# Three raw-weight buffers and four chain rows instead of two and five, norm factors spread by transposes, and a channel mean by one product

## The chip, the cores and the metric

The kernel runs on one core of one Trainium2 chip. The metric is the device time of one execution in microseconds (us). The core's engines are named as the profile names them: PE is TensorE's matmuls and PEld its weight loads, DVE is VectorE, ACT is ScalarE, POOL is GpSimd, SP is the engine whose queue issues most of the DMAs.

## The reference, cut to what matters

A decoder trunk of two layers works on 1024 tokens with 1024 channels, all in 32-bit floats. Each layer does, cut to its steps:

```python
a = rmsnorm(h, norm_mix_pre[i])
u = a @ w_in[i]                      # q, k, v, indexer's qi, ki, wi, and the two other groups
y_attn = dsa_sparse_attention(...)   # per query: the 256 best keys by the indexer, softmax over them
y_conv = conformer_conv(...)         # GLU, depthwise conv of 31 taps, LayerNorm, swish, pointwise
y_pool = multiscale_pool(...)
h = h + rmsnorm(concat(y_attn, y_conv, y_pool) @ w_out[i], norm_mix_post[i])
m = relu(rmsnorm(h, norm_mlp_pre[i]) @ w_up[i]) ** 2
h = h + rmsnorm(m @ w_down[i], norm_mlp_post[i])
h = h + sigmoid(h @ ple_gate[i]) * (p[i] @ ple_proj[i])
```

An rmsnorm divides each token by the root of the mean of its squares over 1024 channels. The LayerNorm in `conformer_conv` takes away the mean over 256 channels first.

## The kernel before, in words

Activations lie with channels on the partitions and tokens along the row, so a norm needs a sum over partitions. The tokens are done in two halves of 512. The work is a list of eight phases (layer, half, kind): `win` is the first projection of a half, `m` all from the output projection to the gate. Two things run beside each other in the program.

**The dense stream.** A phase is a run of units. A unit multiplies one block of weights, 1024 x 128, with eight activation tiles (`slot`), each split into a high and a low part, and sums 24 matmuls into one bank (`pd`, a ring of three): high by high (line 243), high by low (248), low by high (249; where activations are fresh, 245 and 246 in the other order). `prepare` fetches the raw weights by DMA into a buffer of the ring `wraw` (line 199, 512 KB on SP's queue), and for each half of the block ACT copies the high part (`whi`, line 204) and POOL subtracts it to get the low part (`wlo`, line 205). `whi` and `wlo` hold four halves each, two units. In an `m` phase eight units of `w_up` fill eight slots, whose split is done by ACT (line 260) and DVE (line 261) after the square (lines 981, 982), and eight units of `w_down` read all eight slots; this happens four times. I call the change from one to the other an up-down edge: the first matmul of `w_down` needs slots that were split a moment ago.

**The chain.** Attention, convolution and pooling of a half run as generators beside the dense units (`run`, `advance`), a share of them for each unit. For the second half of a layer attention goes in three stages. `index` scores the keys. `select` finds the 256th largest score of each query by bisecting, first over the upper and then over the lower 16 bits, 31 steps in all; in each step ACT counts for key blocks 1 and 2 (line 683) and DVE for blocks 0 and 3 (line 669), each count writes flags that nobody reads into a buffer taken from a ring, and DVE then works out the next threshold from the four counts (lines 687 to 689). For the second half that ring is `row`, and two of its buffers hold the packed scores through the whole stage. Then `attend` does softmax and products (transposes on line 789, products with the values on lines 797 and 798), two heads at a time, with the probabilities of two pairs in `row` buffers. The convolution takes its buffers from `row` too. Attention's results go by DMA to `mixS` (line 812); at the start of an `m` phase the chain of that half has been drained, and POOL's queue loads eight slots from `mixS` (line 923).

**The order.** The code says which instructions there are, and which buffer each use gets: a ring hands out the buffer that was put back first. A scheduler with its own model of time then sets the order on each engine, and adds the waits for buffers that are used again. Engines run their instructions in that order.

**Norm factors.** `token_sums` brings the sums of squares onto partitions, one column per 128 tokens (line 298, 128x1 results). A tiny DVE and a POOL instruction make the factor, and `spread` (line 303) brings it back along the row on all partitions, by four products of a broadcast column with the identity. `rms` does all of that. The convolution's mean uses `token_sums`, a DVE scaling (line 551) and `spread`.

Of the kernel before, what the change touches and what calls it, by code (L numbers as in the profile page):

```python
# [8 lines left out]
F32 = mybir.dt.float32  # L9
# [7 lines left out]
OP = mybir.AluOpType  # L17

P = 128
# [67 lines left out]
def tile_trunk(ctx: ExitStack, tc: tile.TileContext, xT, pT, pos, vecs, invf, cinv,  # L87
               win, wout, wup, wdown, wgate, wple, wcp, outT):
    nc = tc.nc
    te, ve, sc, gp, sy = nc.tensor, nc.vector, nc.scalar, nc.gpsimd, nc.sync  # L90
    side = ["dense"]

    const = ctx.enter_context(tc.tile_pool(name="const", bufs=1))
# [26 lines left out]


    slots = Ring("slot", 16, [P, 2, HALF], F32R)
    wraw = Ring("wraw", 2, [P, 8, P])
    whi = Ring("whi", 4, [P, 4, P], F32R)
    wlo = Ring("wlo", 4, [P, 4, P], F32R)
    dtmp = Ring("dtmp", 11, [P, HALF])
    ctmp = Ring("ctmp", 5, [P, HALF])
    cmat = Ring("cmat", 6, [P, HALF], F32R)
    rows = Ring("row", 5, [P, 1088])
    qst = Ring("qst", 2, [P, 4, P], F32R)  # L130
    idx_t = [const.tile([P, (5 + j) * P], F32, name=f"idx{j}") for j in range(4)]
    kd = const.tile([P, 2, S], F32R, name="kd")
# [6 lines left out]
    def tiny(name, n=4, dt=F32, bufs=4):  # L139

        key = name + side[0][0]
        if key not in tinies:
            tinies[key] = [small.tile([P, n], dt, name=f"{key}{i}") for i in range(bufs)]
        tinies[key].append(tinies[key].pop(0))
        return tinies[key][-1]
# [8 lines left out]
    ident = const.tile([P, P], F32, name="ident")  # L154
    ve.tensor_scalar(ident, jp, 0.0, None, op0=OP.is_equal)
    ones = const.tile([P, 1], F32, name="ones")
    ve.memset(ones, 1.0)
    mhalf = const.tile([P, 4], F32, name="mhalf")
    ve.memset(mhalf, -0.5)
    hb = const.tile([P, DEPTH, 2], F32, name="hb")  # L160
# [133 lines left out]
    def token_sums(ps, srcs):  # L294

        for j in range(4):
            for i, src in enumerate(srcs):
                te.matmul(ps[:, j:j + 1], src[:, j * P:(j + 1) * P], ones, start=i == 0, stop=i == len(srcs) - 1)  # L298

    def spread(ps, t4):  # L300

        for j in range(4):
            te.matmul(ps[:, j * P:(j + 1) * P], t4[:, j:j + 1].to_broadcast([P, P]), ident, start=True, stop=True)

    def rms(ps, srcs, n, eps, other=None):

        token_sums(other or ps, srcs)
        v = tiny("rv")
        ve.tensor_scalar(v, (other or ps)[:, :4], 1.0 / n, eps, op0=OP.mult, op1=OP.add)
        r = tiny("rr")  # L310
        gp.tensor_tensor(r, v, mhalf, op=OP.pow)
        spread(ps, r)
# [12 lines left out]
    def win_phase(l, hf, xs, sq):  # L325
# [53 lines left out]
        for name in win_order(l, hf):  # L379
# [14 lines left out]
            elif kind == "P":  # L394
# [4 lines left out]
                if c == 1:  # L399
                    bg.append(((l, hf), conv_pool(l, hf)))  # L400
# [54 lines left out]
    def conv_pool(l, hf):  # L455
# [39 lines left out]
        for c in range(2):  # L495
# [20 lines left out]
            ps = banks.get()  # L516
# [28 lines left out]
        ps = banks.get()  # L545
        both = ctmp.get()
        gp.tensor_tensor(both, acc[:, 0], acc[:, 1], op=OP.add)
        token_sums(ps, [both])
        ctmp.put(both)
        mu = tiny("mu")  # L550
        ve.tensor_scalar(mu, ps[:, :4], 1.0 / 256, None, op0=OP.mult)
        spread(ps, mu)
        sq = [ctmp.get(), ctmp.get()]
        for c in range(2):
            ve.tensor_tensor(acc[:, c], acc[:, c], ps, op=OP.subtract)
# [22 lines left out]
        for o in range(2):  # L578
            ps = banks.get()
# [584 lines left out]
```

## Time and profile before

| what | value |
|---|---|
| time, median of 3 runs | 2843.78 us (2837.95 to 2844.03) |
| time of the profiled execution | 2843.85 us |
| its span, first to last instruction | 2842.1 us |
| PE busy | 2720.5 us, 96% of the span |
| DVE, ACT, POOL busy | 1747.6, 1548.1, 1418.0 us |
| mean granted clock of TensorE | 0.985 of full speed |

Matmuls are pipelined, so the time of one in the profile is longer than the distance to the next, and the busy time counts overlaps once. A clock of 0.50 is TensorE's lower level, 1.2 GHz in place of 2.4.

### The profile page before, as it was taken

Reading aid. Unit: us, or ns where it says so; the run is one execution under the profiler, and the core shown is the slowest. Engines: PE = TensorE matmul, PEld = TensorE weight load, DVE = VectorE, ACT = ScalarE, POOL = GpSimd, SP = SyncE. Lnnn points to the kernel's source line nnn. Section 1 sums busy time; section 2 is a strip of 40 time slices with the busy share of each in tenths; the row PEclk is TensorE's granted clock in tenths of the full one; section 3 lists DMA queues with packets and bytes.
Section 4 is the critical chain, followed back from the end, with each engine's and each line's share of the span. In section 5 each row is a group of like instructions: output and inputs, shape, how many; then the busy total and the mean of one; then the engine's idle time right before and its main releaser. Section 6 shows DMA issues by size and latency. Waiting matters only on the chain.

```text
span 2842.1 us, 37724 instructions
## 1 busy us (share of the span) xinstructions
PE 2720.5 (96%) x12648; PEld 2242.8 (79%) x12648; DVE 1747.6 (61%) x3473; ACT 1548.1 (54%) x2932; POOL 1418.0 (50%) x1161
## 2 busy tenths in 40 slices
PE   7899989999999999899999989999999999999998
PEld 6677777887888878778788777888878878788886
DVE  7969679788447775965822467587985561511123
ACT  5347667775567535766334423677757654533343
POOL 4655425444334665544544755444443356544446
PEclk9999999999999999999999999999999999999999
DMA  5676554422343576533333547534223354423233
GB/s 189 198 192 218 153 134 148 112 85 90 93 115 106 159 238 187 162 116 102 114 104 104 184 152 238 152 116 108 97 79 98 104 164 138 155 97 99 98 97 122
DMA packets 195666, 384.90 MB, mean 135 GB/s; under 512 B 17424, under 2 KB 76944, under 8 KB 195472
## 3 DMA queue, kind: packets, MB, share of 16 engines
q1 hardware_dynamic: 138192, 330.58, 35.7%
q0 software_dynamic: 57280, 51.91, 8.7%
q8 instruction: 100, 1.64, 0.3%
q14 instruction: 94, 0.77, 0.1%
HBM read 307.97 MB, written 74.45 MB: 135 GB/s over the span
## 4 chain that ended last, share of the span: by engine, by line
PE 72%; DVE 16%; DMA 5%; ACT 3%; issue 3%; POOL 1%; SPq 0%; POOLq 0%; DVEq 0%; ACTq 0%
PE pd L243 20%; PE pd L249 20%; PE pd L248 20%; PE bank L601 5%; DVE bank L537 2%; PE bank L789 2%; DVE dtmp L875 1%; DVE row L669 1%; DVE slot L261 1%; DMA row<-cpS 1%; PE bank L798 1%; PE bank L797 1%; DVE cmat L261 1%; PE pd L298 1%; DVE dtmp L261 1%
## 5 line engine op out<-in xcount | busy, mean ns | idle before, releaser
L205 POOL TENSOR_TENSOR wlo<-wraw,whi 128x512 fp32r<-128x512 f32 x824 | 1094.7, 1334 | 1180.6 <-ACT whi L204 1115.4
L243 PE MATMUL pd<-slot,whi 128*128 128x512 f32 x3296 | 1306.8, 397 | 50.7 <-DVE slot L261 14.5
L248 PE MATMUL pd<-slot,whi 128*128 128x512 f32 x3168 | 1246.0, 393 | 4.6 <-DVE slot L261 2.7
L249 PE MATMUL pd<-slot,wlo 128*128 128x512 f32 x3168 | 1241.9, 393 | 4.1 <-POOL wlo L205 4.0
L204 ACT ACTIVATE whi<-wraw 128x512 fp32r<-128x512 f32 x824 | 511.1, 627 | 731.3 <-PE pd L248 499.0
L243 PEld LDWEIGHTS pd<-slot,whi 128*128 128x128 f32 x3296 | 625.6, 190 | 188.4 <-DVE slot L261 16.6
L249 PEld LDWEIGHTS pd<-slot,wlo 128*128 128x128 f32 x3168 | 600.0, 189 | 130.9 <-POOL wlo L205 7.5
L248 PEld LDWEIGHTS pd<-slot,whi 128*128 128x128 f32 x3168 | 601.1, 190 | 125.8 <-DVE slot L266 3.9
L601 PE MATMUL bank<-kd,qst 128*128 128x512 f32 (+3 forms) x1024 | 261.5, 360 | 10.6 <-DVE mxc L767 3.7
L646 DVE SCALAR_TENSOR_TENSOR idx<-bank,wiT,idx 128x512 f32<-128x512 f32 (+3 forms) x300 | 189.3, 652 | 94.7 <-ACT bank L642 90.7
L601 PEld LDWEIGHTS bank<-kd,qst 128*128 128x128 f32 x1024 | 181.7, 192 | 46.6 <-DVE idx L646 6.8
L642 ACT ACTIVATE bank<-bank 128x512 f32<-128x512 f32 (+2 forms) x320 | 153.8, 506 | 90.0 <-PE bank L601 85.2
L981 DVE SCALAR_TENSOR_TENSOR pd<-pd,rb 128x512 f32<-128x512 f32 x112 | 77.7, 694 | 183.2 <-PE pd L249 183.2
L995 DVE TENSOR_TENSOR yT<-yT,pd 128x512 f32<-128x512 f32 x96 | 65.5, 684 | 197.8 <-PE pd L249 197.5
L537 DVE SCALAR_TENSOR_TENSOR bank<-row,vec,bank 128x512 f32<-128x512 f32 x232 | 162.1, 746 | 0.5
L669 DVE TENSOR_SCALAR_CACHE_REDUCE row<-row,cc 128x640 f32<-128x640 uint16 (+1 forms) x124 | 133.5, 1077 | 14.5 <-ACT row L683 12.6
L683 ACT ACTIVATE row<-row,cc 128x768 f32<-128x768 uint16 (+1 forms) x124 | 121.5, 983 | 18.0 <-DVE cc L689 15.3
L767 DVE CUSTOM_DVE_ANT_0 row<-bank,idx 128x512 f32<-128x512 f32 (+3 forms) x160 | 91.4, 591 | 64.0 <-PE bank L601 60.6
L261 DVE TENSOR_TENSOR cmat<-bank,cmat 128x512 fp32r<-128x512 f32 (+1 forms) x160 | 97.9, 631 | 49.4 <-ACT cmat L260 43.8
L261 DVE TENSOR_TENSOR slot<-pd,slot 128x512 fp32r<-128x512 f32 x112 | 76.6, 685 | 51.3 <-ACT slot L260 51.1
L982 ACT ACTIVATE pd<-pd 128x512 f32<-128x512 f32 x112 | 65.2, 582 | 72.8 <-DVE pd L981 72.7
L775 ACT ACTIVATE row<-row,nmc 128x384 f32<-128x384 f32 (+5 forms) x96 | 84.2, 878 | 27.8 <-DVE nmc L771 21.0
(216 smaller groups left out, 2828.7 us busy)
## 6 DMA issues: line engine op xcount, KB each, us to landing
wraw<-wup SPq DMA_DIRECT2D x128, 512.0 KB, 3.3
wraw<-wdown SPq DMA_DIRECT2D x128, 512.0 KB, 3.3
wraw<-win SPq DMA_DIRECT2D x84, 512.0 KB, 4.2
qiS<-dtmp SPq DMA_DIRECT2D x64, 256.0 KB, 2.5
slot<-mixS POOLq DMA_DIRECT2D x32, 512.0 KB, 7.0
wraw<-wgate SPq DMA_DIRECT2D x32, 512.0 KB, 3.6
qst<-qiS POOLq DMA_DIRECT2D x48, 256.0 KB, 3.7
hS<-yT SPq DMA_DIRECT2D x48, 256.0 KB, 3.6
```

The lines of the kernel that those rows point to most:

```text
L204: sc.activation(hi, r, AF.Copy)
L205: gp.tensor_tensor(lo, r, hi.bitcast(F32), op=OP.subtract)
L243: te.matmul(ps, wh, xh, start=i == 0, stop=False)
L248: te.matmul(ps, wh, xl, start=False, stop=False)
L249: te.matmul(ps, wl, xh, start=False, stop=i == n - 1)
L261: ve.tensor_tensor(lo, src, hi.bitcast(F32), op=OP.subtract)
L537: ve.scalar_tensor_tensor(acc[:, c] if k == TAPS - 1 else pa, src, w, pa, op0=OP.mult, op1=OP.add)
L601: te.matmul(ps[:, :n1 - n0], q, kd[:, k, k0 + n0:k0 + n1], start=k == 0, stop=k == 1)
L642: sc.activation(r, r, AF.Relu)
L646: ve.scalar_tensor_tensor(at, r, w, at, op0=OP.mult, op1=OP.add)
L669: ve.tensor_scalar(flags[:, :Ws[j]], of[j], t, None, op0=op, op1=OP.add, accum_out=dst[:, j:j + 1])
L683: sc.activation(flags[:, :Ws[j]], of[j], AF.Sign, scale=-1.0, bias=c[:, j:j + 1], accum_out=cnt[:, j:j + 1])
```

## The change

The ring `wraw` gets a third buffer and the ring `row` loses its fifth. `spread` asks for transposes in place of matmuls. The convolution's mean over 256 channels is one matmul of the summed channels with a 128 x 128 tile of 1/256, whose result already stands on all partitions; the sums by token, the scaling and a spread fall away there.

```diff
-    wraw = Ring("wraw", 2, [P, 8, P])
+    wraw = Ring("wraw", 3, [P, 8, P])
...
-    rows = Ring("row", 5, [P, 1088])
+    rows = Ring("row", 4, [P, 1088])
...
+    mean256 = const.tile([P, P], F32, name="mean256")
+    ve.memset(mean256, 1.0 / 256)
...
     def spread(ps, t4):
 
         for j in range(4):
-            te.matmul(ps[:, j * P:(j + 1) * P], t4[:, j:j + 1].to_broadcast([P, P]), ident, start=True, stop=True)
+            te.transpose(ps[:, j * P:(j + 1) * P], t4[:, j:j + 1].to_broadcast([P, P]), ident)
...
         both = ctmp.get()
         gp.tensor_tensor(both, acc[:, 0], acc[:, 1], op=OP.add)
-        token_sums(ps, [both])
+        te.matmul(ps, mean256, both, start=True, stop=True)
         ctmp.put(both)
-        mu = tiny("mu")
-        ve.tensor_scalar(mu, ps[:, :4], 1.0 / 256, None, op0=OP.mult)
-        spread(ps, mu)
```

The scheduler decides anew, and the order of all engines differs. In the rows below the changed kernel's lines are one or two off: its lines 668, 682, 686 to 688 are 669, 683, 687 to 689 before, 206 and 207 are 204 and 205, 922 is 923, 1017 is 1018.

The first place is one step of the bisection in `select` of the first layer's second half, on ACT and on DVE. Before, ACT's counts and DVE's counts, with the tile that takes the flags first:

```order
L683 ACTIVATE row_123,cntc_1386<-row_126,cc_1426 128x768
L683 ACTIVATE row_125,cntc_1386<-row_124,cc_1426 128x896
...
L669 TENSOR_SCALAR row_127,cntc_1386<-row_126,cc_1426 128x640
L687 TENSOR_SCALAR bank_141<-cc_1426 128x4
L669 TENSOR_SCALAR row_123,cntc_1386<-row_124,cc_1426 128x1024
L688 TENSOR_TENSOR gec_1431<-cntc_1386,bank_141 128x4
L689 SCALAR_TENSOR_TENSOR cc_1427<-gec_1431,bank_141 128x4
```

The same step in the changed kernel:

```order
L682 ACTIVATE row_126,cntc_1376<-row_125,cc_1416 128x768
L682 ACTIVATE row_127,cntc_1376<-row_124,cc_1416 128x896
...
L668 TENSOR_SCALAR row_126,cntc_1376<-row_125,cc_1416 128x640
L668 TENSOR_SCALAR row_127,cntc_1376<-row_124,cc_1416 128x1024
L687 TENSOR_TENSOR gec_1421<-cntc_1376,bank_141 128x4
L688 SCALAR_TENSOR_TENSOR cc_1417<-gec_1421,bank_141 128x4
```

Before, DVE's first count has a flags buffer of its own (127) and its second takes the one of ACT's first count (123). Now both of DVE's counts write where ACT's counts of the same step write (126 and 127).

The second place is the convolution's mean on PE in the first layer's first half. Before, among the dense matmuls, its eight instructions stand in two fours, with 19 other rows between:

```order
L298 MATMUL bank_141<-ones,ctmp_113 128x1 x4
...
L303 MATMUL bank_141<-ident,muc_1213 128x128 x4
```

In the changed kernel one row does that work:

```order
L250 MATMUL pd_139<-slot_84,whi_96 128x512
L251 MATMUL pd_139<-slot_84,wlo_100 128x512
L245 MATMUL pd_139<-slot_85,whi_96 128x512
L550 MATMUL bank_141<-ctmp_114,mean_155 128x512
L250 MATMUL pd_139<-slot_85,whi_96 128x512
```

Eight instructions became one, of 512 columns. The other spreads keep their four rows each and their places among the neighbours.

The third place is on POOL at the end of phase (second layer, first half, `m`): the loads of attention's results for the last phase, among the gate's units (1018 is the gate's addition, 205 the low parts of the weights). Before:

```order
L876 TENSOR_TENSOR yT<-dtmp_108,dtmp_107 128x512
L205 TENSOR_TENSOR wlo_99<-wraw_92,whi_95 128x512
L923 DMA slot_87<-mixS 128x2x512
...
L923 DMA slot_90<-mixS 128x2x512
L205 TENSOR_TENSOR wlo_98<-wraw_91,whi_94 128x512
L1018 TENSOR_TENSOR yT<-yT,dtmp_110 128x512
```

In the changed kernel:

```order
L1017 TENSOR_TENSOR yT<-yT,dtmp_106 128x512
L207 TENSOR_TENSOR wlo_100<-wraw_92,whi_96 128x512
L207 TENSOR_TENSOR wlo_101<-wraw_92,whi_97 128x512
L922 DMA slot_87<-mixS 128x2x512
...
L922 DMA slot_90<-mixS 128x2x512
L1017 TENSOR_TENSOR yT<-yT,dtmp_107 128x512
L207 TENSOR_TENSOR wlo_98<-wraw_93,whi_94 128x512
```

Before, all eight of the gate's additions stand behind the four loads; now five stand ahead of them and three behind. On PE the last product of the second layer's attention moves with them: before, 180 dense matmuls stand between it and the first matmul of the last phase, now 65.

## Rows read from the trace of the kernel before

**Rows 1.** The page's busy times of each engine over the whole span.

```profile
PE 2720.5 (96%) x12648; PEld 2242.8 (79%) x12648; DVE 1747.6 (61%) x3473; ACT 1548.1 (54%) x2932; POOL 1418.0 (50%) x1161
```

**Rows 2.** PE's waits, whole span: us in total, times, longest.

```profile
PE pd L243 <- DVE slot L261: 14.5, 6, 4.3
PE pd L243 <- ACT whi L204: 11.2, 6, 7.0
```

**Rows 3.** Line 303's records: ns min/median/max, first and last start, forms.

```profile
L303 PE MATMUL pd<-ident,rrd x64: 270/275/581, 28.4 to 2456.0; 128*128 128x128 f32 x64
L303 PE MATMUL bank<-ident,muc x32: 271/275/275, 208.7 to 1754.2; 128*128 128x128 f32 x32
```

**Rows 4.** PE's timeline, three runs of like records: start, us, instruction, count.

```profile
203.42 0.95 PE L298 MATMUL bank<-ones,ctmp 128*128 128x1 f32 x8
...
208.69 1.05 PE L303 MATMUL bank<-ident,muc 128*128 128x128 f32 x8
...
2292.32 1.25 PE L789 MATMUL bank<-ident,row 128*128 128x128 f32 x10
```

**Rows 5.** Timelines of DVE and ACT, one bisecting step; idle time in brackets.

```profile
544.66 0.88 DVE L669 TENSOR_SCALAR_CACHE_REDUCE row<-row,cc 128x640 f32<-128x640 int16 x1
545.78 1.28 DVE L669 TENSOR_SCALAR_CACHE_REDUCE row<-row,cc 128x1024 f32<-128x1024 int16 x1 [0.16 <-ACT row L683]
547.56 0.88 DVE L669 TENSOR_SCALAR_CACHE_REDUCE row<-row,cc 128x640 f32<-128x640 int16 x1
...
544.72 0.94 ACT L683 ACTIVATE row<-row,cc 128x768 f32<-128x768 int16 x1 [0.33 <-DVE cc L689]
545.65 1.03 ACT L683 ACTIVATE row<-row,cc 128x896 f32<-128x896 int16 x1
546.59 0.18 ACT L683 ACTIVATION_READ_ACCUMULATOR row<-row,cc 128x1 f32 x1
```

**Rows 6.** PE's waits in 530:660, 660:700 and 2090:2115; then DVE's timeline.

```profile
PE pd L243 <- DVE slot L261: 0.7, 1, 0.7
...
PE pd L243 <- DVE slot L261: 6.4, 3, 4.3
...
PE pd L243 <- DVE slot L261: 4.0, 1, 4.0
PE pd L248 <- DVE slot L261: 2.7, 1, 2.7
...
681.70 3.08 DVE L752 TENSOR_TENSOR_SCAN row<-row 128x896 f32<-128x896 f32 x1
```

**Rows 7.** Windows: us, busy of each engine (count), granted clock, DMA share, GB/s.

```profile
538.00:660.00 122.00, 121.35 (x538) 100.43 (x537) 109.02 (x272) 97.75 (x190) 55.80 (x44) 1.00 0.29 96
2103.50:2106.90 3.40, 3.40 (x11) 2.71 (x10) 3.40 (x7) 0.72 (x2) 0.00 (x0) 0.50 0.00 0
683.50:690.30 6.80, 4.89 (x12) 3.82 (x13) 6.80 (x10) 0.83 (x2) 0.00 (x0) 0.50 0.10 40
```

**Rows 8.** Timelines around the last phase's start, and how long its loads take.

```profile
2321.64 0.28 PE L798 MATMUL bank<-cmat,vst 128*128 128x256 f32 x1
...
2326.12 3.58 SPq L812 DMA_DIRECT2D mixS<-ctmp x2
...
2332.01 2.89 POOL L923 DMA_DIRECT2D slot<-mixS  x4
...
DMA to landing us min/median/max: 5.5/6.7/9.5
...
2368.12 0.39 PE L243 MATMUL pd<-slot,whi 128*128 128x512 f32 x1
```

**Rows 9.** ACT's waits for raw weights (whole span), one of them, PE's wait after it.

```profile
ACT whi L204 <- DMA wraw<-win: 61.5, 22, 8.8
...
2344.58 1.15 ACT L204 ACTIVATE whi<-wraw 128x512 fp32r<-128x512 f32 x2 [7.62 <-DMA wraw<-wgate]
...
PE pd L243 <- ACT whi L204: 0.8, 1, 0.8
```

## The prediction

> **What bounds the kernel now.** I read the busy times first. PE is busy for 2720.5 of 2842.1 us, the next engine for 1747.6 [rows 1], so PE is the bound, and every column that it need not work counts unless PE would only wait instead. About 120 us of the span PE stands still, so the second view is what it waits for. No single wait is large: the largest named are DVE's splits of activations, 14.5 us in six waits, and weights not yet copied by ACT, 11.2 us in six [rows 2]. The third view is the records of the lines that the diff touches [rows 3, 4], and the fourth is the stage in which the ring `row` is used hardest, the bisecting [rows 5]. There DVE is busy for 109 and ACT for 98 of 122 us, while PE is busy for 121.35 with dense units alone [rows 7]: the chain runs at its own pace beside a full PE. So a slower step there costs nothing by itself; what matters is where the chain's later work then lands.
>
> **The spreads.** A spread is four instructions, but line 303 left two records for each: the mean's four spreads have 32 records and not 16 [rows 3]. Eight such records take 1.05 us and the last one alone 0.275, so they start (1.05 - 0.275) / 7 = 0.111 us apart [rows 3, 4]. The transposes of line 789 have the same shape and type and one record each, (1.25 - 0.275) / 9 = 0.108 us apart [rows 4]. A spread then takes 4 x 0.108 = 0.43 in place of 8 x 0.111 = 0.89 us. There are 64 records for rrd [rows 3], the rows for rrn and rrc read x64 and x32, so 160 / 8 = 20 spreads stay: 20 x 0.46 = 9.2 us less. Whether PE is full or waits for the factor, the same 0.46 us lies on its way. The bounds are 0, if the changed instruction still takes two records, and 9.2; I take 9, since its operands have the same shape and type as line 789's. The Trainium skill (Perfetto Trace Analysis, Transposes) says to use a transpose for what is logically one, as it skips the arithmetic. That alone names no saved time, and by it the term could be 0; the row shows that the record is halved too, and the trace decides.
>
> **The mean.** Four times, eight records of line 298, and eight of line 303 go [rows 4]. With the same 0.275 for the last one, line 298's start (0.95 - 0.275) / 7 = 0.10 us apart, so 0.80 + 0.89 = 1.69 us go. One product of 512 columns in full 32-bit comes. No row has that shape. As two records at the dense stream's distance (122 us / 538 = 0.227 us [rows 7]) it would take 0.45; scaled from line 303 by columns, 8 x 0.111 = 0.89. I take 0.89, since line 303 is the same kind of product. That is 0.80 us less, 3.2 in all (up to 5.0). The Trainium skill (FP8 and Floating Point Precision, TensorE Precision Notes) gives a true 32-bit product four passes; at the dense distance that would be 4 x 0.227 = 0.91 us, an estimate that agrees with the upper bound. DVE's scaling and one trip between engines leave the chain too, at a place where PE works on dense units: nothing.
>
> **The row ring.** In a step now, DVE's first count starts at 544.66, its second waits 0.16 us for ACT's first count and starts at 545.78, and the next step starts at 547.56: 2.90 us. ACT's second count ends at 546.59 + 0.18 = 546.77 [rows 5]. By the changed order both of DVE's counts write the flags of ACT's counts, so the second can't start before 546.77 instead of 545.78: about 1.0 us more per step, 31 us per stage, twice. Behind the waiting count on DVE stand the splits and sums of dense units. The order now puts them between steps, and a unit takes 24 x 0.227 = 5.4 us with three `pd` banks, so a wait of 1 us is covered. The price if all of it were on the path is 62 us. The Trainium skill (Perfetto Trace Analysis, Optimization Strategy) reads a gap that repeats on the engine that should be saturated as too few buffers. By that rule the change makes such gaps, but on DVE; the engine that should be saturated is PE, and it is covered here [rows 7].
>
> What becomes late is the stage's tail: scans of up to 3.1 us each on DVE [rows 6]. Now the tail meets an up-down edge in both layers, and PE waits for the last splits 6.4 us (660:700) and 4.0 + 2.7 us (2090:2115). At the edge that falls inside the bisecting the wait is only 0.7 us [rows 6]. After the waits the clock falls to 0.50, for 3.4 us with PE busy throughout, and for 6.8 us of which 4.9 us are busy [rows 7]; half of 3.4 and 4.9 is 4.1 us. So 13.1 + 4.1 = 17.2 us hang on this coincidence. With the stage 31 us (some 6 units) longer, the same edges fall inside the last steps of the bisecting and the tail beside `w_down`, whose units need one sum each from DVE. If both edges then cost 0.7 us, 15.8 us are gained. If the tail's scans delay `pd` banks there, or edges now meet DVE waiting for ACT, nothing is. I take the middle, 8 us less.
>
> **The end of attention, second layer.** The chain's lateness must be caught up by the last phase, which needs all of attention. Now the last product is at 2321.64, the write to `mixS` starts at 2326.12, the loads at 2332.01, and they land 5.5 to 9.5 us after issue: with 2.89 us for four and a median of 6.7, at 2341.6. The phase's first matmul is at 2368.12 [rows 8], so 26.5 us are spare. In the changed order 65 dense matmuls, 65 x 0.227 = 14.8 us, follow the last product; the way to the landing takes 2341.6 - 2321.6 = 20 us now, or 2332.0 + 0.7 + 5.5 - 2321.6 = 16.6 for the first load. So PE waits 2 to 5 us there. A clock drop like the one above may add 1.7. I take 4 us more, bounds 0 and 9. In the first layer the drained chain has long been done when the second half's `m` phase begins: nothing. Four row buffers also let a head start only when an older pair's products are done; `attend` is squeezed into fewer units than before, and I put 2 us more for small waits of PE, bounds 0 and 10.
>
> **The third raw buffer.** ACT's waits for raw weights are long (61.5 us for `win` alone), but ACT has slack. Where a fetch issued late holds ACT 7.62 us PE waits 0.8 us right after [rows 9]. All of PE's waits for `whi` are 11.2 us [rows 2], and most follow ACT's or PE's own work. I take 2 us less, bounds 0 and 6.
>
> **Sum.** -9 - 3 - 8 + 4 + 2 - 2 = -16 us. The profiled execution took 2843.85 us, within 0.1 of the median shown, so 2828 us. What the scheduler shuffles elsewhere I can't price; PE's idle time is some 120 us in small pieces, and I let it move by 8 us either way.
>
> **Rivals.** (a) Only PE's saved columns count, 12 us, and what the edges give is taken by new waits elsewhere: 2843.85 - 12 = 2832, give or take the shuffle, up to 2838. For it speaks that a longer stage must meet other edges; against it the order, which shows the tail clear of them.
> (b) The spreads do not get cheaper, since only arithmetic is skipped, and the edges give little: 2843.85 - 3 - 2 = 2839. Line 789's single records speak against it.
> (c) Slower: attention of the second layer misses the last phase. If `attend` isn't squeezed, it ends 31 us later, 4.5 us past the 26.5 that are spare; if four buffers also stretch each of its 16 pairs of heads by 2 us, 32 us more. PE would then stand for some 36 us with no dense unit left, less 9 + 3 + 8 + 2 = 22 us of the other terms: 2843.85 + 36 - 22 = 2858 us. This decides from 26.5 + 22 = 48 us of lateness at the last product; here it would be 63. Against it: `attend` is paced by the shares that the code gives it, and the order has it back within 65 matmuls.
> (d) All 62 us of the longer stages on the path, 2890: PE's full window speaks against it.
>
> **How the numbers follow.** The forecast, 2828 within 2817 to 2837, has 0.53; (a) 0.2; (b) 0.1; (c) 0.14; (d) 0.03. A measurement of this kernel tells some 0.2%, 5.7 us, from no change. Faster than 2838: the forecast's 0.52, 0.16 of (a) and 0.03 of (b), 0.71. Within: 0.16, the rest of (a) and (b) and a mild (c). Slower: 0.13. The range of 8 in 10 goes from 2815 (the edges and the product of the mean at their better bounds) to 2844, leaving out (c) and (d).
>
> **What the changed profile would show.** Line 303's successor with one record per transpose, 0.108 us apart (right) or two (b). One bisecting step of 3.9 us in place of 2.9, with DVE waiting for ACT twice. No wait of 4 us at the up-down edges near 680 and 2100. A wait of a few us at the last phase's first matmul. Wrong I am if PE's idle time grows by more than PE's work falls, above all if the wait at the last phase is tens of us, or if new waits stand in `attend`.

## Result and profile after

The changed kernel takes 2824.7 us (median of 4 runs, 2822.6 to 2826.2), beside 2841.9 for the kernel before: a ratio of 0.994 [0.9923, 0.9958], 17 us less (12 to 22). The forecast was 2828, 16 less.

The page of the changed kernel, first its busy times, which answer to [rows 1], then its costliest groups (busy time, mean ns | time in which PE or DVE stood still just before them, and what ended most of it):

```profile
span 2824.4 us, 37476 instructions
...
PE 2710.4 (96%) x12512; PEld 2232.7 (79%) x12512; DVE 1763.1 (62%) x3470; ACT 1547.2 (55%) x2930; POOL 1424.8 (50%) x1161
...
L245 PE MATMUL pd<-slot,whi 128*128 128x512 f32 x3296 | 1307.0, 397 | 46.3 <-DVE dtmp L263 9.4
L250 PE MATMUL pd<-slot,whi 128*128 128x512 f32 x3168 | 1248.9, 394 | 0.8 <-DVE slot L268 0.8
L251 PE MATMUL pd<-slot,wlo 128*128 128x512 f32 x3168 | 1246.1, 394 | 0.6 <-POOL wlo L207 0.5
...
L600 PE MATMUL bank<-kd,qst 128*128 128x512 f32 (+3 forms) x1024 | 263.1, 360 | 20.1 <-DVE mxc L766 12.9
...
L668 DVE TENSOR_SCALAR_CACHE_REDUCE row<-row,cc 128x640 f32<-128x640 uint16 (+1 forms) x124 | 133.6, 1078 | 68.4 <-ACT row L682 61.4
```

The same groups on the page of the kernel before (243, 248, 249 are the dense matmuls, 601 the scores, 669 DVE's counts):

```profile
L243 PE MATMUL pd<-slot,whi 128*128 128x512 f32 x3296 | 1306.8, 397 | 50.7 <-DVE slot L261 14.5
L248 PE MATMUL pd<-slot,whi 128*128 128x512 f32 x3168 | 1246.0, 393 | 4.6 <-DVE slot L261 2.7
L249 PE MATMUL pd<-slot,wlo 128*128 128x512 f32 x3168 | 1241.9, 393 | 4.1 <-POOL wlo L205 4.0
...
L601 PE MATMUL bank<-kd,qst 128*128 128x512 f32 (+3 forms) x1024 | 261.5, 360 | 10.6 <-DVE mxc L767 3.7
...
L669 DVE TENSOR_SCALAR_CACHE_REDUCE row<-row,cc 128x640 f32<-128x640 uint16 (+1 forms) x124 | 133.5, 1077 | 14.5 <-ACT row L683 12.6
```

The span fell by 17.7 us: PE worked 10.1 us less, and stood still for 2824.4 - 2710.4 = 114.0 in place of 121.6, 7.6 less. Of the standing, the dense matmuls lost 59.4 - 47.7 = 11.7 us, and the scores of attention took 20.1 - 10.6 = 9.5 us more: most of what the dense stream no longer waits for, attention waits for. DVE's counts wait for ACT for 61.4 us where it was 12.6.

The busy time can't be read as columns alone, because the clock differs. The profile's mean granted clock, before and then in the changed kernel:

```profile
core 0: 2842.1 us, clock 0.985
core 0: 2824.4 us, clock 0.982
```

Summed over all stretches at 0.50, PE works for 68.1 us at the lower level before, and for 81.6 us in the changed kernel. Half of the difference, 6.7 us, is work drawn out by the clock. So with the same time at the lower clock (I say: at one clock) PE's work would have fallen by some 16.8 us, of which 6.7 came back.

**Spreads and mean.** Records of the spread's line for one factor, and of the mean's product (ns min/median/max), and then three rows of PE's timeline, the product with the dense matmul behind it, and a spread:

```profile
L305 PEld LDWEIGHTS pd<-ident,rrd x32: 132/136/230, 29.3 to 2438.6; 128*128 128x128 f32 x32
L305 PE MATMUL pd<-ident,rrd x32: 270/272/476, 29.3 to 2438.7; 128*128 128x128 f32 x32
...
L550 PE MATMUL bank<-ctmp,mean x8: 590/591/697, 204.0 to 1735.3; 128*128 128x512 f32 x8
```

```profile
204.01 1.02 PE L550 MATMUL bank<-ctmp,mean 128*128 128x512 f32 x2
204.46 0.80 PE L250 MATMUL pd<-slot,whi 128*128 128x512 f32 x1
...
220.01 0.60 PE L305 MATMUL bank<-ident,rrc 128*128 128x128 f32 x4
```

The 64 records of [rows 3] are 32 now, one per transpose. Four take 0.60 us, (0.60 - 0.272) / 3 = 0.109 us apart, as forecast. The mean's product is two records that start 1.02 - 0.591 = 0.43 us apart, 0.86 us for both; 0.89 was taken.

**The bisecting.** Two of DVE's timeline rows inside a step, which answer to [rows 5], and the first and last count of the first layer's stage, in the changed kernel and then before:

```profile
654.36 0.88 DVE L668 TENSOR_SCALAR_CACHE_REDUCE row<-row,cc 128x640 f32<-128x640 uint16 x1 [1.18 <-ACT row L682]
...
655.39 1.28 DVE L668 TENSOR_SCALAR_CACHE_REDUCE row<-row,cc 128x1024 f32<-128x1024 uint16 x1
```

```profile
L668 DVE TENSOR_SCALAR_CACHE_REDUCE row<-row,cc x62: 866/1072/1282, 539.8 to 696.0; 128x640 f32<-128x640 uint16 x16, 128x1024 f32<-128x1024 uint16 x16, 128x640 f32<-128x640 int16 x15, 128x1024 f32<-128x1024 int16 x15
...
L669 DVE TENSOR_SCALAR_CACHE_REDUCE row<-row,cc x62: 867/1072/1283, 539.1 to 657.1; 128x640 f32<-128x640 uint16 x16, 128x1024 f32<-128x1024 uint16 x16, 128x640 f32<-128x640 int16 x15, 128x1024 f32<-128x1024 int16 x15
```

The 1.18 us in brackets is DVE's wait, and ACT's count of the same step ends it. The counts of the first layer run from 539.8 to 697.3 us, where they ran from 539.1 to 658.4; in the second layer from 1945.0 to 2103.5, where it was 1957.3 to 2074.7. The stages are 38 and 41 us longer; 31 was forecast. Over its 31 steps the first layer's stage comes to 5.1 us for a step, where it was 3.8: the prediction's 2.9 us were read from one short step, and its 3.9 from that. PE is busy for all of the 157 us from 540 to 697.

**The edges.** PE's waits in 660:760 (the first of the rows) and in 2070:2160 (us in total, times, longest), which answer to [rows 6]:

```profile
PE bank L600 <- DVE mxc L766: 6.6, 1, 6.6
...
PE bank L600 <- DVE mxc L766: 3.7, 1, 3.7
PE pd L245 <- DVE yT L994: 0.9, 1, 0.9
```

The waits for splits at the edges are gone, and PE stands 6.6 and 3.7 us at another place. PE's timeline there, then DVE's:

```profile
725.07 0.39 PE L251 MATMUL pd<-slot,wlo 128*128 128x512 f32 x1
732.05 0.69 PE L600 MATMUL bank<-kd,qst 128*128 128x128 f32 x2 [6.60 <-DVE mxc L766]
732.54 0.73 PE L245 MATMUL pd<-slot,whi 128*128 128x512 f32 x1
733.08 0.63 PE L250 MATMUL pd<-slot,whi 128*128 128x512 f32 x1
733.50 0.63 PE L251 MATMUL pd<-slot,wlo 128*128 128x512 f32 x1
```

```profile
721.28 5.25 DVE L751 TENSOR_TENSOR_SCAN row<-row 128x896 f32<-128x896 f32 x2
726.45 2.08 DVE L752 SCALAR_TENSOR_TENSOR row<-row,needc,row 128x896 f32<-128x896 f32 x1
...
730.25 1.14 DVE L753 SCALAR_TENSOR_TENSOR idx<-idx,thrc,row 128x896 f32<-128x896 f32 x1
731.32 0.68 DVE L766 CUSTOM_DVE_ANT_0 row<-bank,idx 128x512 f32<-128x512 f32 x1
```

A score stands next on PE, and its bank is free only when DVE has taken a softmax maximum (line 766), which comes behind the tail's scans. All dense matmuls after that score wait too. The clock falls here, from 728.3 on and so while PE still stands, and at the second layer's wait, as it did at the edges in [rows 7] (us busy and count by engine, PE first; the granted clock is the 0.50, the lower level of 1.2 GHz):

```profile
728.30:738.50 10.20, 6.45 (x17) 5.29 (x18) 9.48 (x26) 2.56 (x6) 0.00 (x0) 0.50 0.00 0
2134.60:2141.40 6.80, 5.38 (x14) 4.32 (x15) 6.80 (x19) 1.92 (x4) 0.40 (x1) 0.50 0.00 0
```

That is 17.0 us at the lower level (PE busy 11.8), where it was 10.2 us (busy 8.3) before.

**The last phase and the raw weights.** PE's wait in 2320:2400, then ACT's groups of waits for raw weights in the whole run, which answer to [rows 8, 9]:

```profile
PE pd L245 <- DMA slot<-mixS: 1.2, 2, 0.8
...
ACT whi L206 <- DMA wraw<-wup: 5.1, 2, 4.0
ACT whi L206 <- DMA wraw<-wgate: 5.0, 2, 4.0
ACT whi L206 <- DMA wraw<-win: 3.4, 1, 3.4
```

At the start of the last phase PE waits for 1.2 us; 2 to 5 were forecast. ACT's waits for raw weights are 13.5 us, where those for `win` alone were 61.5.

### The profile page after: what moved, and what is told of

It reads as the page before. It is cut to its first block, busy times and chain, and to the rows that moved or that the text cites. A ratio compares the mean times of both kernels' runs of the same rounds, so it can differ in the third digit from the quotient of the medians.

```text
span 2824.4 us, 37476 instructions
## 1 busy us (share of the span) xinstructions
PE 2710.4 (96%) x12512; PEld 2232.7 (79%) x12512; DVE 1763.1 (62%) x3470; ACT 1547.2 (55%) x2930; POOL 1424.8 (50%) x1161
## 5 line engine op out<-in xcount | busy, mean ns | idle before, releaser
L245 PEld LDWEIGHTS pd<-slot,whi 128*128 128x128 f32 x3296 | 627.2, 190 | 185.0 <-issue 11.8
L600 PE MATMUL bank<-kd,qst 128*128 128x512 f32 (+3 forms) x1024 | 263.1, 360 | 20.1 <-DVE mxc L766 12.9
L668 DVE TENSOR_SCALAR_CACHE_REDUCE row<-row,cc 128x640 f32<-128x640 uint16 (+1 forms) x124 | 133.6, 1078 | 68.4 <-ACT row L682 61.4
L262 ACT ACTIVATE cmat<-bank 128x512 fp32r<-128x512 f32 (+1 forms) x160 | 84.0, 548 | 37.1 <-PE bank L788 28.8
```

The source lines that it names most:

```text
L245: te.matmul(ps, wh, xh, start=i == 0, stop=False)
L600: te.matmul(ps[:, :n1 - n0], q, kd[:, k, k0 + n0:k0 + n1], start=k == 0, stop=k == 1)
L668: ve.tensor_scalar(flags[:, :Ws[j]], of[j], t, None, op0=op, op1=OP.add, accum_out=dst[:, j:j + 1])
```

## Experiments

All ratios are to the kernel before, run on the same chip; 0.001 is 2.8 us. Of two kernels compared by their ratios, each has an interval of 2 to 5 us either way (the changed kernel's own is 5), so their difference has one of 3 to 6.

**Each part alone.** `spread` by transposes and nothing else:

```diff
-            te.matmul(ps[:, j * P:(j + 1) * P], t4[:, j:j + 1].to_broadcast([P, P]), ident, start=True, stop=True)
+            te.transpose(ps[:, j * P:(j + 1) * P], t4[:, j:j + 1].to_broadcast([P, P]), ident)
```

> Only the spreads become transposes (24 of them, the mean's four too); rings and mean as before. Theory of the prediction: 24 spreads of 0.46 us less on PE, 11 us less than before (2831), give or take the scheduler's shuffle of 5 us, since the spread's time lies on PE's way. Rival, the change's gain is the rings' (the edges moved clear of the bisecting's tail): under 5 us less. Rival, transposes are only relabelled matmuls: no change, two records each.

The ratio is 0.9985 [0.9976, 0.9994], 4.3 us less (1.7 to 6.8). PE is busy for 2711.1 us, 9.4 less, where 11 were forecast; the time did not follow in full. In the profiled execution (2836.12 us, 2.8 below the median of the twelve) PE stands for 122.9 us, only 1.3 more than before. The mean by one product alone:

```diff
-        token_sums(ps, [both])
+        te.matmul(ps, mean256, both, start=True, stop=True)
...
-        spread(ps, mu)
```

> Only the mean by one product; spreads as matmuls, rings as before. Theory: four times 1.69 us of records go and 0.89 come: 3 us less than before (2839), which a measurement hardly tells from none. Rival: the mean's shorter trip lets the convolution end sooner and moves waits: 8 us or more either way.

The ratio is 0.997 [0.9958, 0.9983], 8.5 us less (4.8 to 11.9), where columns alone would give 3.2. PE's busy time is not lower (2722.8); the span is 2836.1, so PE stands 113.3 us in place of 121.6. What is gained in this execution is in waits. That the busy time did not fall is for the most part the clock again: 76.9 us of work at the lower level, in place of 68.1. Then the rings alone, `wraw` 3 with `row` 4, and `row` 4 with two raw buffers:

```diff
-    wraw = Ring("wraw", 2, [P, 8, P])
+    wraw = Ring("wraw", 3, [P, 8, P])
...
-    rows = Ring("row", 5, [P, 1088])
+    rows = Ring("row", 4, [P, 1088])
```

> Only the two rings: three raw buffers, four rows. Theory of the prediction: the edges' 8 us less, 4 and 2 us more for the last phase and for attention, 2 us less by the raw buffer: 4 us less than before, between 12 less and 8 more. Rival, the rings carry the change: 10 us or more less. Rival, the longer bisecting is paid: slower than before.

> Only the rows cut from five to four; two raw buffers. Theory: the bisecting takes 3.9 us or more per step instead of 2.9, PE stays full there, the waits at the two up-down edges go and smaller ones come: 2 us less than before, between 10 less and 10 more. Rival, the third raw buffer pays for a loss by the rows: 5 us or more slower than before here, while both rings together are not slower.

The ratio is 0.9974 [0.9964, 0.9984] for both rings, 7.4 us less, and 0.9985 [0.9973, 0.9996] for `row` 4 alone, 4 less. So the fifth row buffer was worth nothing here, and the third raw buffer beside it some 3 us, within the noise of the pair. The three parts alone add to 4.3 + 8.5 + 7.4 = 20 us, the whole gave 17: within their intervals they add up.

**One part taken back.** The changed kernel with `wraw` 2, and the changed kernel with matmuls in `spread`:

```diff
-    wraw = Ring("wraw", 3, [P, 8, P])
+    wraw = Ring("wraw", 2, [P, 8, P])
```

> The changed kernel with two raw buffers again. Theory: the third buffer was worth 2 us, so 2827, hardly to be told from 2825; ACT's waits for raw weights are back to some 130 us, which PE does not feel. Rival, the third buffer brought what the columns don't explain: 5 us or more slower than the changed kernel.

> The changed kernel with the spreads as matmuls again. Theory: 20 x 0.46 = 9 us slower than the changed kernel (2834), PE busy up by 9 us. Rival, as the spreads alone gained only 4 us: 2 to 5 us slower, the rest of the columns fills idle time.

The ratios are 0.9953 [0.994, 0.9966] and 0.9954 [0.994, 0.9967], each some 4 us above the changed kernel's 0.994, within their intervals of it. With matmuls PE is busy 8.6 us longer (2719.0) but stands for 2829.5 - 2719.0 = 110.5 us, 3.5 less. Alone, the spreads give 4.3 of the 11 us of their columns; taken back, some 4 of 9, with an interval that holds both 0 and 9.

**The order shuffled.** The scheduler's order depends on numbers in the code. One of them was changed, which changes nothing that is computed:

```diff
-RATES = (1.171, 1.114, 0.558, 0.766, 0.722, 0.567, 0.741, 0.946)
+RATES = (1.160, 1.114, 0.558, 0.766, 0.722, 0.567, 0.741, 0.946)
```

> The changed kernel with one number of the planner moved by 1% (the chain's share in the first phase, 1.171 to 1.160), which changes no work and only lets the scheduler decide otherwise. It measures what a mere reshuffle is worth: the prediction allowed 8 us either way. If it moves by 3 us or less, the differences of 4 us and more in the other runs are the edits' own; if by 5 or more, they can't be read as such.

The ratio is 0.9937 [0.9925, 0.9949], 1 us from the changed kernel; the same edit on the best kernel (below) moved it by 4 us. A difference of 4 us between two orders is therefore no evidence on a part by itself.

**Flags that don't go round.** In the bisecting ACT's counts get one buffer for their flags, and DVE's another, so that DVE never waits for a buffer that ACT writes:

```diff
+            mine = {}
...
-                    flags = spare.get()
+                    flags = mine.get("dve") or spare.get()
...
-                        flags = spare.get()
-                        sc.activation(flags[:, :Ws[j]], of[j], AF.Sign, scale=-1.0, bias=c[:, j:j + 1],
+                        sc.activation(mine["act"][:, :Ws[j]], of[j], AF.Sign, scale=-1.0, bias=c[:, j:j + 1],
...
+            mine.update(act=spare.get(), dve=spare.get())
```

> The changed kernel, but in the bisecting ACT's counts all write one flags buffer and DVE's counts another, so that neither engine waits for the other's flags; four rows as in the changed kernel. Theory of the prediction: a step takes 2.9 us again, the stage is some 35 us shorter, its tail meets the up-down edges near 680 and 2090 again, and the time is up to 10 us above the changed kernel's (2825 to 2835). Rival, the longer stage is a cost that the change pays for: below the changed kernel by 3 us or more (under 2822). Rival, neither matters: the same within 3 us.

The time is 2813.2 us (4 runs), a ratio of 0.9903 [0.9889, 0.9917]: 28 us below the kernel before and some 10 below the changed one. Its mean clock, rows of its page, and PE's waits in 1900:2160:

```profile
core 0: 2812.2 us, clock 0.985
...
PE 2702.1 (96%) x12512; PEld 2226.6 (79%) x12512; DVE 1748.7 (62%) x3470; ACT 1551.9 (55%) x2930; POOL 1424.5 (51%) x1161
...
L600 PE MATMUL bank<-kd,qst 128*128 128x512 f32 (+3 forms) x1024 | 262.0, 360 | 9.1 <-DMA qst<-qiS 4.8
...
L669 DVE TENSOR_SCALAR_CACHE_REDUCE row<-row,cc 128x640 f32<-128x640 uint16 (+1 forms) x124 | 133.7, 1078 | 1.9
```

```profile
PE pd L250 <- DVE slot L263: 3.4, 1, 3.4
PE pd L245 <- ACT slot L262: 1.6, 1, 1.6
```

DVE's waits inside the steps went from 68.4 to 1.9 us, and the scores' waits from 20.1 to 9.1, the size of before. The counts run from 537.3 to 655.1 us in the first layer: the stage is short again. My theory had a short stage bring back the old edges, at 2825 to 2835 us; that is refuted. Waits for splits are back (3.4 + 1.6, and 2.7 in 640:760), but smaller than those of [rows 6]. The Trainium skill (Perfetto Trace Analysis, Optimization Strategy) takes a gap that repeats on the engine that should be saturated as a possible sign of too few buffers; the gap here was on DVE and not on PE, so I had set it aside. With three raw buffers a buffer for each engine took the gap away and the kernel got faster. With two, below, the same edit gives nothing.

How the gap cost PE time is shown in part. The profiled execution's span is 12.2 us shorter than the changed kernel's. PE stands for 110.1 us in place of 114.0, 3.9 less; the other 8.3 us are busy time with the same 12512 records, and 7.8 of them are the clock: 66.0 us of work at the lower level in place of 81.6. By place, 8 us are gained in the first layer's first `m` phase, around the bisecting (622.1 us from its first dense matmul to the next phase's, in place of 630.2), and 4 are lost in the second layer's (598.6 in place of 594.8); the rest lies in other phases. The two shuffled builds differ likewise in these phases, by 5 us gained and 4 lost.

Is that the flags, or the third raw buffer with them? The same flags with `wraw` 2 and `row` 4, with `wraw` 2 and `row` 5, in the kernel before, and in the best kernel with the changed number:

> e5 with two raw buffers and four rows. It splits the swap: against e5 it shows the third raw buffer alone, against e9 the fifth row alone. Theory from e6 (two raw buffers 3 us slower): 2816. Rival: the same as e5.

> Transposes, mean by one product and the own flags buffers of e5, with the rings of the kernel before (two raw, five rows). If the ring swap is worth nothing once the flags don't make engines wait, the time is e5's within 3 us (2813). If the third raw buffer is what makes e5 fast, it is 5 us or more above e5. If the fifth row helps attention, it is 3 us or more below e5.

> The kernel before with own flags buffers for ACT and DVE, nothing else. If what e5 gained on the changed kernel is only the undoing of the wait that four rows make, nothing or 1 to 2 us is gained here, since five rows made DVE wait only 0.16 us per step: 2840. If own flags buffers are worth something of their own, it is 5 us or more below before.

> e5 with the planner's number moved by 1% as in e8: what a reshuffle alone does to e5. In e8 it gave 3 us less. If it again moves by 3 us or less, e5's 12 us below the changed kernel are the flags' own.

The ratios are, in this order, 0.9965 [0.9953, 0.9977], 0.9966 [0.9956, 0.9977], 0.9982 [0.9973, 0.9991] and 0.9917 [0.9903, 0.9931]. The shuffle moves the best kernel by 4 us, more than the 3 that I had allowed, so the size of the flags' gain is open by as much. The first build was forecast at 2816 us, and took 2834.5. With own flags the third raw buffer is worth (0.9965 - 0.9903) x 2843 = 17 us, or 14 if the shuffled build is taken for three buffers; with shared flags it was 4. Own flags are worth 10 us with three raw buffers (6 between the two shuffled builds), 5 in the kernel before, and nothing in the changed kernel with two (0.9965 beside 0.9953). The fifth row is again worth nothing (0.9966 beside 0.9965). Nor does a short stage by itself clear the scores: with own flags, two raw buffers and five rows they wait 24.0 us, 13.9 of them for a maximum.

The busy times in 176:250 and 250:322 (PE first), of the build with own flags and two raw buffers, and then of the one with three:

```profile
176.00:250.00 74.00, 67.23 (x290) 53.12 (x289) 60.70 (x140) 38.36 (x82) 40.12 (x36) 0.95 0.61 183
250.00:322.00 72.00, 68.19 (x324) 54.67 (x323) 61.38 (x217) 46.42 (x124) 35.17 (x31) 1.00 0.68 198
```

```profile
176.00:250.00 74.00, 73.68 (x332) 60.22 (x331) 65.04 (x178) 45.71 (x106) 45.64 (x41) 0.98 0.65 193
250.00:322.00 72.00, 71.93 (x354) 59.97 (x353) 62.90 (x202) 50.54 (x125) 34.91 (x32) 1.00 0.65 193
```

PE is busy for 135.4 of 146 us with two and 145.6 with three: 10 of the 17 us are lost there, well ahead of the bisecting. Two of PE's waits in 176:322 of the first of these builds, the longest and the one for copied weights:

```profile
PE bank L600 <- DMA qst<-qiS: 3.6, 1, 3.6
...
PE pd L245 <- ACT whi L206: 1.1, 1, 1.1
```

So PE does not lose its time there by waiting for weights: the longest wait is for an operand of the scores. In the build with five rows it is another, 5.2 us for a maximum, so there is no single cause to name. The kernel before has two buffers as well, and PE is busy for 73.7 + 68.4 = 142.1 us in the same stretch. With two raw buffers, the cheaper spreads and the mean together it is 135 to 137 us, with shared flags (136.6) as with own ones and five rows (137.1); in the builds with two buffers and one of the parts it is 142 to 144. So the loss belongs to the orders made with two buffers and the cheaper spreads and mean together, not to two buffers as such, and not to the flags. With shared flags the kernel wins some of it back elsewhere; where, I did not take apart.

## Why the prediction was right, and where its terms were off

**The total held; its halves agree in part by luck.** PE's busy time fell by 10.1 us (9 + 3 forecast), and its standing by 7.6 (8 - 4 - 2 + 2 = 4 forecast). But the 10.1 are 16.8 less at one clock and 6.7 more by the clock. Of the 16.8 the prediction has 12; what the other 5 us are is open (the rings alone, which change no column, give 3.1 at one clock). For the clock over the whole run it has no term. Nor is the time gained where the prediction put it. The two `m` phases with the edges and the bisecting took 630.2 and 594.8 us, where it was 628.2 and 600.0. Most came in the first layer's second `m` phase, 525.6 us in place of 537.2, where PE works 6.7 us at the lower clock in place of 18.9: 11.6 of the span's 17.7 us, in a phase to which the prediction gave no wait. The records behave as the steps said: one per transpose, 0.109 us apart, and two for the product. Rival (b), spreads that are not cheaper, is refuted by the records, rivals (c) and (d) by the time and by a last phase that waits for 1.2 us.

**The spreads, -9, were mis-sized.** They measured -4.3 (1.7 to 6.8) alone, where 11 would be theirs, and some -4 in the whole, with a wide interval. The records are right; the step that failed is "the same 0.46 us lies on its way" wherever PE is. Where the rest went is not shown: in the whole, PE stands 3.5 us more with transposes than with matmuls, alone only 1.3 more, and a shuffle can move as much.

**The mean, -3, was mis-sized the other way:** -8.5 (4.8 to 11.9) alone. I put the shorter trip through DVE and `spread` at nothing since PE works on dense units there. The gain lies in PE's waits, which fell by 8.3 us in that build's profiled execution. Whether it is the shorter trip or the new order is open; a shuffle moved other builds by 1 and 4 us.

**The edges, -8, came to nothing.** The coincidence was read rightly: the waits of 6.4 and 4.0 + 2.7 us for splits are gone, and the step that failed is the middle taken between 15.8 us and nothing. What I did not price is what the tail meets next: attention's first scores, whose banks wait for a maximum behind the tail's scans, 6.6 and 3.7 + 0.9 us, 11.2 in place of 13.1. `row` 4 alone shows the same, 6.8 and 5.5 us, so these waits come with the shorter ring. The lower clock lasted longer around them (PE busy 11.8 us at 0.50 in place of 8.3, half of the difference is 1.7 us), which takes back the 1.9 us that were left. This is the mechanism of rival (a), "what the edges give is taken by new waits elsewhere", inside a total that is the forecast's.

**The bisecting** was off by a quarter: stages 38 and 41 us longer, not 31. DVE waits for ACT once in most steps (61.4 us in 55 waits, 1.1 us each, as in the row at 654.36), not twice. The waits grew by 61.4 - 12.6 = 48.8 us, 24 of each stage's 38 to 41; what fills the rest I did not take apart. "A wait of 1 us is covered" held while the steps ran; after them came the scores' waits. With own flags, the other parts unchanged, the kernel is 10 us faster.

**The last phase, +4,** was 1.2 as a wait, and the small waits in `attend`, +2, don't stand apart from the 11.2 above. The last phase as a whole is 3.3 us longer (470.5 us), with 6.8 us of work at the lower clock and none before.

**The third raw buffer, -2 (0 to 6),** was 3 to 4 in this kernel, by two pairs of runs, neither clear of its interval. That it is worth 14 to 17 once the flags are parted was outside my bounds. Most of ACT's waits for raw weights went, and the forecast rightly put most of that at nothing.

Terms off by 2 to 8 us each, in both directions, made a total off by one: luck has a large share in it. Not settled are the rest of the 17 us of the third buffer with own flags, and why own flags give nothing with two raw buffers. Five rows and three raw buffers together weren't tried.

## What to carry to other kernels

When a stall is to move, name the next instruction on the bound engine that waits behind the thing that is late: here the splits got free, and the next in line, attention's scores, paid nearly as much. Buffers that only take results nobody reads still order engines; try a buffer for each engine before the ring is made smaller (here 5 to 10 us in three pairs of builds, nothing in a fourth). When busy time changes, compare the time at each clock level before it is read as columns. Where a scheduler makes the order anew, time each part alone and a shuffle that computes the same, and don't ascribe a difference of the shuffle's size to a part.

## What the runs showed of the hardware

A transpose's weight load is shorter as well: 136 ns, in place of the 190 of the matmul with the same operands, which in the kernel before read

```profile
L303 PEld LDWEIGHTS pd<-ident,rrd x64: 185/190/333, 28.4 to 2455.9; 128*128 128x128 f32 x64
```

The starts are as far apart as before (0.109 and 0.111 us), so the spread's gain is that of its halved records. And a wait of PE cost more than its own length: around the 6.6 us of standing the clock was granted at 0.50 for 10.2 us, with 6.45 us of work in them, and dense matmuls started 0.43 us apart in place of 0.23. Half of that work, 3.2 us, came on top of the wait. Over the whole run such stretches make 6.7 us between the two kernels, as much as a part of the change is worth.
